# A hybrid encoder layer: near scores multiplied in pairs, a shorter second norm, three subtractions queued later

## The chip, the cores and the metric

The kernel runs on one core of one Trainium2 chip. The core has five engines with a queue each, worked off in order: TensorE (PE; its weight loads are shown apart as PEld), VectorE (DVE), ScalarE (ACT), GpSimd (POOL) and SyncE (SP), which here only issues transfers. TensorE writes into PSUM, a small memory of eight banks of 2 KB per partition; the other data lie in SBUF, and large ones in device memory. The metric is the device time of one launch in microseconds (us), lower is better.

## The reference

The input x has 1024 positions of 1024 features. One layer is computed, in float32:

```
u = RMSNorm(x);  p = u @ W_in               split into attention and delta-rule parts
A: 8 heads of 64, chunks of 64 positions; each chunk attends to itself and the 8 chunks before it
   scores = q k^T / 8 + bias[clipped distance];  softmax;  o_att = RMSNorm(P v)
B: 4 heads of 128: causal convolution, SiLU, gated delta-rule recurrence over chunks, gated RMSNorm
h = x + concat[o_att, B] @ W_out
h = h + relu(RMSNorm(h) @ W1)^2 @ W2        W1 is 1024 x 4096, W2 is 4096 x 1024
```

The second RMSNorm divides each position by sqrt(mean(h^2) + EPS). Because the activation is relu squared, the kernel can multiply its result by 1 / (mean(h^2) + EPS) after the activation instead: a plain reciprocal, no root.

## The kernel before, in words

The positions are columns and the features are rows of 128. Each float32 operand of the large products is split into a high part (a cast on ScalarE, L149) and a low part (a subtraction on VectorE or GpSimd, L150), and each product is three matmuls: high by high, high by low, low by high.

The work goes through these stages. The projections by W_in come first (to about 363 us). Then attention and the delta rule run side by side (to about 575 us): two Python generators hand out pieces in turn, and each piece's instructions enter the program in that order. Then comes the product with W_out (to 661 us), the first feed-forward product (to 974 us) and the second (to the end). The order of each engine's queue is not the program's order alone: a planner at compile time works through the program with a model of durations, gives each engine the ready instruction that stands first in the program, and adds the semaphore waits. The kernel bends that order with two means. `tc.issue_after(ins)` queues what is traced inside it behind `ins` on the same engine, with no wait added; `tc.high_priority()` lets it go before other ready work.

**Attention.** A unit is one group of four heads (g), one block of 128 positions (t) and one pair of heads (pp). `score` (from L795) first handles the near keys, that is the own block of 128 and the one before it. For each of the two heads, `product` writes two matmuls per block of keys into one half of one PSUM bank (t_sb), and VectorE adds the bias, writes the result to SBUF and takes the negated minimum of the negated scores in the same instruction (L810, t_nm). Then come the far keys, one bank per head (t_sa, L819), with the near minimum as start value, and ScalarE's exponentials (L825, L828). `value` transposes them on TensorE (t_tpb, t_tpa), copies them out (t_tb, t_ta) and multiplies by the values (t_o).

**The second norm.** `norm_col` (from L1036) loads the sums of squares, already added up over the rows of features except for the last 128, and sums these by matmuls with a column of ones, one column of result per block of 128 positions (hcol). VectorE turns that into mean plus EPS (L1045) and takes the reciprocal (L1047) into r_col, behind an addition of the second column block (held). `norm_row` (L1049) spreads r_col along rows by matmuls with an identity (hrow), and ScalarE copies them out as r2 (L1055), with which every result of the first feed-forward product is multiplied (emit, L1097).

**The second feed-forward product.** `ff2` computes seven products instead of eight per round (Strassen's scheme in Winograd's form), in four rounds over the rows of W2 (kb from 0 to 3), in the order p1, p5, p2, p3, p6, p7, p4. Each product takes sums or differences of quarters of the operands as input, made on VectorE:

```
prep5: s1 = a21 + a22;    b11 = b12 - b11        (L1263, L1264)
prep3: s1 = s1 - a11;     a12 = a12 - s1         (L1268, L1269)
prep6: b11 = b22 - b11                           (L1273)
prep7: a21 = a11 - a21;   b12 = b22 - b12        (L1277, L1278)
prep4: b21 = b11 - b21                           (L1282)
```

Each runs twice per product, on pieces of 128 x 1024 (i is 0 or 1). Then the operands are split, and 48 matmuls follow (L1185). Names such as p50b_l say: product 5, round 0, operand b, low part. The results are added to y on VectorE (L1253) or copied on ScalarE (L1251).

Of the kernel before, what the change touches and what calls it, by code (L numbers as in the profile page):

```python
# [8 lines left out]
F32 = mybir.dt.float32  # L9
F32R = mybir.dt.float32r  # L10
AF = mybir.ActivationFunctionType
ALU = mybir.AluOpType
AX = mybir.AxisListType

P = 128
SEQ = 1024
DM = 1024
NKT = DM // P
NT = SEQ // P
# [9 lines left out]
EPS = 1e-6  # L29
# [17 lines left out]
def hymba_kernel(  # L47
# [20 lines left out]
    nc = tc.nc  # L68
    PS = bass.MemoryType.PSUM

    cpool = ctx.enter_context(tc.tile_pool(name="cpool", bufs=1))
# [29 lines left out]
    def bank(pool, name):  # L101
        return pool.tile([P, 512], F32, tag="bk", name=name)
# [4 lines left out]
    ones = cpool.tile([P, P], F32, name="ones")  # L107
# [3 lines left out]
    warm = bank(ps_o, "warm")  # L111
    for i in range(WARM):
        nc.tensor.matmul(warm[:, 0:P], ones, ones, start=True, stop=True)
    ident = cpool.tile([P, P], F32, name="ident")
    make_identity(nc, ident)
    tri_u = mpool.tile([P, P], F32, name="tri_u")
# [31 lines left out]
    def split(src, hi, lo, hi_eng, lo_eng):  # L148
        a = nc.scalar.copy(hi, src) if hi_eng is nc.scalar else hi_eng.tensor_copy(hi, src)  # L149
        return a.ins, lo_eng.tensor_tensor(lo, src, hi.bitcast(F32), ALU.subtract).ins  # L150
# [21 lines left out]
    r_col = cpool.tile([P, NT], F32, name="r_col")  # L172
# [535 lines left out]
    def attention(after):  # L708
# [74 lines left out]
        def product(g, T, i, bk, off, ka, kb):  # L783

            q = T["q"]
            cost = 0
            for hf in range(2):
                a, b = max(ka, 4 * hf), min(kb, 4 * hf + 4)
                if a >= b:
                    continue  # L790
                k = keys[g][hf][i]
                o = bk[:, off + (a - ka) * P:off + (b - ka) * P]
                c = slice((a - 4 * hf) * P, (b - 4 * hf) * P)
                for m in range(2):
                    nc.tensor.matmul(o, q[m][:, i * P:(i + 1) * P], k[:, c], start=(m == 0), stop=(m == 1))  # L795
                cost += max(214, (b - a) * 107)
            return cost

        def score(g, t, pp):
            T = tiles[g, t]  # L800
            n, k0, kb, nm = (T[k] for k in ("n", "k0", "kb", "nm"))
            wa, wb = (kb - k0) * P, (t + 1 - kb) * P
            cost = 0
            bk = bank(ps_a, f"{n}_sb{pp}")
            sb = page("u" if g or t > 1 else "wr", f"{n}_pb{pp}")
            for e in range(2):
                i = 2 * pp + e
                c = slice(e * 256 + 256 - wb, e * 256 + 256)
                cost += product(g, T, i, bk, c.start, kb, t + 1)
                nc.vector.tensor_tensor_reduce(sb[:, c], bk[:, c], new[g][pp][:, c], -1.0, 3.0e38,  # L810
                                               ALU.add, ALU.min, nm[:, 4 + i:5 + i])
            sa = [None, None]
            if wa:
                for e in range(2):
                    i = 2 * pp + e
                    bk = bank(ps_a, f"{n}_sa{i}")
                    cost += product(g, T, i, bk, 0, k0, kb)
                    sa[e] = page("u", f"{n}_pa{i}")
                    nc.vector.tensor_tensor_reduce(sa[e][:, 0:wa], bk[:, 0:wa], old[g][i][:, 384 - wa:384], -1.0,  # L819
                                                   nm[:, 4 + i:5 + i], ALU.add, ALU.min, nm[:, i:i + 1])  # L820
            for e in range(2):
                i = 2 * pp + e
                c = slice(e * 256 + 256 - wb, e * 256 + 256)
                m = nm[:, i:i + 1] if wa else nm[:, 4 + i:5 + i]
                nc.scalar.activation(sb[:, c], sb[:, c], AF.Exp, bias=m, scale=-1.0,  # L825
                                     accum_out=T["sums"][:, 4 + i:5 + i])
                if wa:
                    nc.scalar.activation(sa[e][:, 0:wa], sa[e][:, 0:wa], AF.Exp, bias=m, scale=-1.0,  # L828
                                         accum_out=T["sums"][:, i:i + 1])
            T["s"][pp] = sa, sb  # L830
            return cost
# [80 lines left out]
        for i in range(len(units) + lag + late):  # L912
            if i < len(units):
                g, t, pp = units[i]
# [8 lines left out]
            if lag <= i < len(units) + lag:  # L923
                g, t, pp = units[i - lag]
# [3 lines left out]
            if i >= lag + late:  # L928
                g, t, pp = units[i - lag - late]
# [69 lines left out]
    def ff1(R, started, psw, pools):  # L999
# [4 lines left out]
        r2 = pools["r2"][0].tile([P, 2, TH], F32, tag="r2", name="r2", bufs=1)  # L1004
        begun, held = {}, []
# [31 lines left out]
        def norm_col():  # L1037

            acc = page2("ut4", "acc")
            nc.sync.dma_start(out=acc, in_=sq_dr)  # L1040
            ps = psw.tile([P, 1024], F32, tag="bk", name="hcol")
            for q in range(NT):
                nc.tensor.matmul(ps[:, q:q + 1], acc[:, q * P:(q + 1) * P], ones[:, 0:1], start=True, stop=True)
            with tc.issue_after(held[-1][2]):
                m = nc.vector.tensor_scalar(r_col, ps[:, 0:NT], 1.0 / DM, EPS, ALU.mult, ALU.add)  # L1045
                with tc.issue_after(m.ins), tc.high_priority():
                    nc.vector.reciprocal(r_col, r_col)  # L1047

        def norm_row():  # L1049

            ps = psw.tile([P, 1024], F32, tag="bk", name="hrow")
            for q in range(NT):
                nc.tensor.matmul(ps[:, q * P:(q + 1) * P], r_col[:, q:q + 1].broadcast_to([P, P]), ident,
                                 start=True, stop=True)
            nc.scalar.copy(r2.rearrange("p a t -> p (a t)"), ps)  # L1055

        def block(sb):
            def lw(tag, name, kh, c):
# [102 lines left out]
    def ff2(psw, pools):  # L1161
# [7 lines left out]

        y = {i: [wide(t, 0), wide(t, 1)] for i, t in y.items()}  # L1170
        y[7] = [page2("y7", f"y7_{i}") for i in range(2)]
        side = [0]

        def load_h(t, j, hf, m):
            nc.sync.dma_start(out=two(t), in_=h_dr[j, hf, :, 2 * m:2 * m + 2, :])
# [1 line left out]
        def product(name, prep, by_rows=False):  # L1177
            t = "AB"[side[0]]
            side[0] ^= 1
            ps = [psw.tile([P, 1024], F32, tag="bk", name=f"{name}{m}") for m in range(4 if by_rows else 2)]  # L1180
            def step(i, k, q):
                (ah, al), (bh, bl) = ops[i]
                s = slice(k * 512 + q * P, k * 512 + (q + 1) * P)
                for m, (l, r) in enumerate(((ah, bh), (ah, bl), (al, bh))):
                    nc.tensor.matmul(part(ps[q], 0) if by_rows else part(ps[q // 2], q % 2), l[:, s], part(r, k),  # L1185
                                     start=(i + k + m == 0), stop=(i + k + m == 4))

            ops = []
            for i in range(2):
                ab = []  # L1190
                for o, src in zip("ab", prep(i)):
                    hi = page2("h" + t, f"{name}{o}{i}_h", F32R)
                    lo = page2("l" + t, f"{name}{o}{i}_l", F32R)
                    split(src, hi, lo, nc.scalar, nc.vector)
                    ab.append((hi, lo))
                ops.append(ab)
                if not by_rows:
                    for k in range(2):
                        for q in range(4):
                            step(i, k, q)  # L1200
            if by_rows:
                for q in range(4):
                    for i in range(2):
                        for k in range(2):
                            step(i, k, q)
            return ps
# [7 lines left out]
        for kb in range(nb):  # L1214
# [18 lines left out]
            a11, b11 = wq("r", "a11", k1, 0), fq("r", "b11", k1, 0)  # L1233
            a21, a22, b12 = wq("rc", "a21", k1, 1), wq("rc", "a22", k2, 1), fq("rc", "b12", k1, 1)
# [11 lines left out]
            s1 = []  # L1246

            def accumulate(i, ps, op=ALU.add):
                for m in range(2):
                    if kb == 0 and i in (1, 5, 6, 7):  # L1250
                        nc.scalar.copy(y[i][m], ps[m])  # L1251
                    else:
                        nc.vector.tensor_tensor(y[i][m], y[i][m], ps[m], op)  # L1253
# [5 lines left out]
            tt = nc.vector.tensor_tensor  # L1259
# [5 lines left out]
                return s1[i], b11[i]  # L1265

            def prep3(i):
                tt(s1[i], s1[i], a11[i], ALU.subtract)  # L1268
                tt(a12[i], a12[i], s1[i], ALU.subtract)  # L1269
                return a12[i], b22[i]  # L1270

# [2 lines left out]
                return s1[i], b11[i]  # L1274

            def prep7(i):
                tt(a21[i], a11[i], a21[i], ALU.subtract)  # L1277
                tt(b12[i], b22[i], b12[i], ALU.subtract)  # L1278
                return a21[i], b12[i]

# [3 lines left out]

            accumulate(1, product(f"p1{kb}", lambda i: (a11[i], b11[i])))
            accumulate(5, product(f"p5{kb}", prep5))
            accumulate(2, product(f"p2{kb}", lambda i: (a12[i], b21[i])))
            if last:
                merge(nc.gpsimd, 2, 1)
# [16 lines left out]
            ps = product(f"p4{kb}", prep4, last)  # L1306
# [3 lines left out]
            for q in range(4):  # L1310
                t = part(y[4][q // 2], q % 2)
# [98 lines left out]
```

## Time and profile before

| | us |
|---|---|
| median of 3 runs | 1286.36 (1286.24 to 1288.97) |
| the profiled execution's own time | 1286.66 |
| its span in the profile | 1284.9 |
| TensorE busy | 1259.1 |
| VectorE busy | 935.3 |
| ScalarE busy | 554.4 |
| GpSimd busy | 292.8 |

The span runs from the first to the last instruction of the profiled execution; its own time also holds the start and end of the launch. Busy time of TensorE counts from a matmul's start to its modelled end, so neighbouring matmuls overlap in it. In rows of the profile in order of time stand start, duration, engine, line, operation, output and inputs by name, shape and count; in brackets the engine's idle time before it and what ended it. Several like instructions in a row are merged into one row with a count.

### The profile page before, as it was taken

What the parts mean: (1) busy time and instruction counts of PE and PEld (TensorE: products, weight loads), DVE (VectorE), ACT (ScalarE), POOL (GpSimd) and SP (SyncE); (2) the same over time, 40 slices, a digit from 0 to 9 for tenths busy, and PEclk for the clock granted to TensorE, in tenths of its full rate; (3) what the DMA queues carried; (4) which work ended last, traced back from release to release, by engine and by line L of the source; (5) the groups of instructions that cost most, each with busy time, mean ns of one, the idle gap of its engine ahead of it and who ended that gap; (6) DMA issues with size and microseconds to landing.
All of it is one profiled execution on the core that took longest, in us unless ns stands there. A gap on an engine that the chain in (4) does not pass through costs nothing.

```text
span 1284.9 us, 18056 instructions
## 1 busy us (share of the span) xinstructions
PE 1259.1 (98%) x6708; PEld 1039.7 (81%) x6708; DVE 935.3 (73%) x1401; ACT 554.4 (43%) x920; POOL 292.8 (23%) x499
## 2 busy tenths in 40 slices
PE   9999999999999999989999999999999999999998
PEld 7778878788888877868877788888887888888886
DVE  7899987655046666863539876776668997897988
ACT  7323132133166654665335455444455443333331
POOL 4425451454024355523310000000000000000034
PEclk9999999999999999999999999999999999999999
DMA  6214354656482642124341433232258633322002
GB/s 223 65 43 142 98 160 118 139 147 164 144 267 81 216 108 75 42 67 163 127 160 37 144 121 125 99 113 99 99 196 323 233 97 101 131 87 95 15 33 98
DMA packets 129288, 160.65 MB, mean 125 GB/s; under 512 B 22832, under 2 KB 71984, under 8 KB 128688
## 3 DMA queue, kind: packets, MB, share of 16 engines
q1 hardware_dynamic: 111104, 137.20, 34.6%
q10 hardware_dynamic: 18096, 22.29, 5.0%
q8 instruction: 53, 0.87, 0.3%
q14 instruction: 35, 0.29, 0.1%
HBM read 111.75 MB, written 47.71 MB: 124 GB/s over the span
## 4 chain that ended last, share of the span: by engine, by line
PE 72%; DVE 9%; DMA 2%; issue 2%; ACT 1%; POOL 1%; POOLq 1%; SPq 0%; DVEq 0%; ACTq 0%
PE q L1089 22%; PE p L1185 20%; PE op L168 5%; PE av_ps L168 3%; PE aq_ps L168 3%; PE g_ps L168 3%; PE t_o L867 2%; PE ak_ps L168 2%; PE t_sb L795 1%; PE t_sa L795 1%; PE t_tpb L846 1%; PE t_tpa L857 1%; PE c_mt L463 1%; PE c_pS L463 1%; DVE ml L150 1%
## 5 line engine op out<-in xcount | busy, mean ns | idle before, releaser
L1257 POOL TENSOR_TENSOR y<-y,y 128x1024 f32<-128x1024 f32 x6 | 19.3, 3242 | 591.7 <-DVE y L1253 572.9
L1253 DVE TENSOR_TENSOR y<-y,p 128x1024 f32<-128x1024 f32 x46 | 55.0, 1214 | 5.4 <-PE p L1185 4.5
L810 DVE CUSTOM_DVE_ANT_0 t_pb<-t_sb,biasn 128x256 f32<-128x256 f32 (+1 forms) x64 | 25.3, 401 | 42.9 <-POOL biasn L722 25.5
L168 PE MATMUL op<-mh,wo_h 128*128 128x512 f32 x128 | 50.3, 393 | 1.0 <-ACT wo_h L149 0.5
L168 PE MATMUL op<-ml,wo_h 128*128 128x512 f32 x128 | 50.1, 391 | 0.0
L168 PE MATMUL op<-mh,wo_l 128*128 128x512 f32 x128 | 48.3, 392 | 0.0
L825 ACT ACTIVATE t_pb<-t_pb,t_nm 128x256 f32<-128x256 f32 (+1 forms) x64 | 31.5, 493 | 22.2 <-DVE t_nm L819 12.1
L968 DVE TENSOR_TENSOR h<-op,op_x 128x512 f32<-128x512 f32 x16 | 10.8, 687 | 29.5 <-PE op L168 29.5
L795 PE MATMUL t_sb<-ks,t_q 128*128 128x256 f32 (+1 forms) x144 | 30.4, 308 | 1.3 <-DMA t_q<-q_dr 1.1
L975 POOL TENSOR_TENSOR op_q<-op_q 128x512 f32<-128x512 f32 x14 | 20.1, 1438 | 47.0 <-ACT op_q L974 46.8
L168 PEld LDWEIGHTS op<-mh,wo_h 128*128 128x128 f32 x128 | 24.1, 188 | 7.6 <-issue 1.0
L819 DVE CUSTOM_DVE_ANT_0 t_pa<-t_sa,biaso,t_nm 128x384 f32<-128x384 f32 (+2 forms) x48 | 26.3, 547 | 4.4 <-PE t_sa L795 2.9
L168 PEld LDWEIGHTS op<-mh,wo_l 128*128 128x128 f32 x128 | 24.0, 188 | 5.2 <-issue 0.2
L168 PEld LDWEIGHTS op<-ml,wo_h 128*128 128x128 f32 x128 | 24.0, 188 | 4.9
L867 PE MATMUL t_o<-t_ta,vt 128*64 128x128 f32 x240 | 26.5, 286 | 1.4 <-DVE t_ta L860 1.1
L828 ACT ACTIVATE t_pa<-t_pa,t_nm 128x384 f32<-128x384 f32 (+2 forms) x48 | 26.4, 550 | 0.1
L168 PE MATMUL g_ps<-uh,wg_h 128*128 128x512 f32 x64 | 25.2, 394 | 1.1 <-ACT wg_h L149 1.1
L795 PE MATMUL t_sa<-ks,t_q 128*128 128x256 f32 (+2 forms) x128 | 25.5, 311 | 0.3 <-DVE t_nm L810 0.3
L168 PE MATMUL g_ps<-uh,wg_l 128*128 128x512 f32 x64 | 25.2, 394 | 0.4 <-POOL wg_l L150 0.4
L168 PE MATMUL dq_ps<-uh,wdq_h 128*128 128x512 f32 x64 | 25.5, 398 | 0.0
L168 PE MATMUL dv_ps<-uh,wdv_l 128*128 128x512 f32 x64 | 25.4, 398 | 0.0
L168 PE MATMUL aq_ps<-waq_h,uh 128*128 128x512 f32 x64 | 25.4, 401 | 0.0
(1103 smaller groups left out, 4351.2 us busy)
## 6 DMA issues: line engine op xcount, KB each, us to landing
wa<-in_w_ff_dram SPq DMA_DIRECT2D x32, 512.0 KB
a<-in_w_ff_dram SPq DMA_DIRECT2D x32, 512.0 KB
b<-f_dr SPq DMA_DIRECT2D x32, 512.0 KB
f_dr<-yy ACTq DMA_DIRECT2D x16, 512.0 KB
t_q<-q_dr SPq DMA_DIRECT2D x30, 256.0 KB
f_dr<-zz ACTq DMA_DIRECT2D x13, 512.0 KB
ks<-k_dr SPq DMA_DIRECT2D x16, 256.0 KB
wo_r<-in_w_out_dram SPq DMA_DIRECT2D x16, 256.0 KB
```

The costliest lines, as they stand in the source:

```text
L168: nc.tensor.matmul(ps, a, b, start=(i == 0), stop=(i == n - 1))
L463: nc.tensor.matmul(ps[:, hs], lhs(h, hs), rhs(h, hs), start=True, stop=True)
L795: nc.tensor.matmul(o, q[m][:, i * P:(i + 1) * P], k[:, c], start=(m == 0), stop=(m == 1))
L810: nc.vector.tensor_tensor_reduce(sb[:, c], bk[:, c], new[g][pp][:, c], -1.0, 3.0e38, ALU.add, ALU.min, nm[:, 4 + i:5 + i])
L819: nc.vector.tensor_tensor_reduce(sa[e][:, 0:wa], bk[:, 0:wa], old[g][i][:, 384 - wa:384], -1.0, nm[:, 4 + i:5 + i], ALU.add, ALU.min, nm[: ...
L825: nc.scalar.activation(sb[:, c], sb[:, c], AF.Exp, bias=m, scale=-1.0, accum_out=T["sums"][:, 4 + i:5 + i])
L828: nc.scalar.activation(sa[e][:, 0:wa], sa[e][:, 0:wa], AF.Exp, bias=m, scale=-1.0, accum_out=T["sums"][:, i:i + 1])
L867: nc.tensor.matmul(po[64 * e:64 * e + 64, pp * P:(pp + 1) * P], vt[k0 + j][:, 64 * h:64 * h + 64], (ta[e] if j < na else tb)[:, c:c + P], ...
L975: nc.gpsimd.tensor_tensor(acc, acc, sq, ALU.add)
L1089: nc.tensor.matmul(part(ps, q), l[:, s], r, start=(k + m == 0), stop=(k == 3 and m == 2))
L1185: nc.tensor.matmul(part(ps[q], 0) if by_rows else part(ps[q // 2], q % 2), l[:, s], part(r, k), start=(i + k + m == 0), stop=(i + k + m == 4))
L1253: nc.vector.tensor_tensor(y[i][m], y[i][m], ps[m], op)
```

## The change

Four edits are made together.

In `score`, the loop over the two heads is cut into two: first both near products are issued, then both minima are taken.

In `norm_col`, a tile epsc filled with EPS * 1024 / 128 (one memset on GpSimd at the start) is multiplied by a matrix of ones, which adds EPS * 1024 to each column of the sum; the nine products become one accumulation. The reciprocal is then taken straight from PSUM, in one VectorE instruction with high priority, and the factor 1024 that the mean lacks is put into ScalarE's copy of the rows.

In `ff2`, each low-part subtraction is remembered, and `early` is the last one of product 5. The subtractions s1 - a11 of product 3 and a11 - a21 of product 7 are queued behind it.

```
+    epsc = cpool.tile([P, NT], F32, name="epsc")
+    nc.gpsimd.memset(epsc, EPS * DM / P)
...
                 cost += product(g, T, i, bk, c.start, kb, t + 1)
+            for e in range(2):
+                i = 2 * pp + e
+                c = slice(e * 256 + 256 - wb, e * 256 + 256)
                 nc.vector.tensor_tensor_reduce(sb[:, c], bk[:, c], new[g][pp][:, c], -1.0, 3.0e38,
                                                ALU.add, ALU.min, nm[:, 4 + i:5 + i])
...
+            nc.tensor.matmul(ps[:, 0:NT], ones, epsc, start=True, stop=False)
             for q in range(NT):
-                nc.tensor.matmul(ps[:, q:q + 1], acc[:, q * P:(q + 1) * P], ones[:, 0:1], start=True, stop=True)
-            with tc.issue_after(held[-1][2]):
-                m = nc.vector.tensor_scalar(r_col, ps[:, 0:NT], 1.0 / DM, EPS, ALU.mult, ALU.add)
-                with tc.issue_after(m.ins), tc.high_priority():
-                    nc.vector.reciprocal(r_col, r_col)
+                nc.tensor.matmul(ps[:, q:q + 1], acc[:, q * P:(q + 1) * P], ones[:, 0:1], start=False, stop=q == NT - 1)
+            with tc.issue_after(held[-1][2]), tc.high_priority():
+                nc.vector.reciprocal(r_col, ps[:, 0:NT])
...
-            nc.scalar.copy(r2.rearrange("p a t -> p (a t)"), ps)
+            nc.scalar.mul(r2.rearrange("p a t -> p (a t)"), ps, float(DM))
...
-                    split(src, hi, lo, nc.scalar, nc.vector)
+                    splits.append(split(src, hi, lo, nc.scalar, nc.vector)[1])
...
             def prep3(i):
-                tt(s1[i], s1[i], a11[i], ALU.subtract)
+                with tc.issue_after(early):
+                    tt(s1[i], s1[i], a11[i], ALU.subtract)
...
             def prep7(i):
-                tt(a21[i], a11[i], a21[i], ALU.subtract)
+                with tc.issue_after(early):
+                    tt(a21[i], a11[i], a21[i], ALU.subtract)
...
             accumulate(5, product(f"p5{kb}", prep5))
+            early = splits[-1]
```

More of the change, by code (lines that the diff above doesn't have):

```diff
@@ L1171, in ff2 @@
         y[7] = [page2("y7", f"y7_{i}") for i in range(2)]
-        side = [0]
+        side, splits = [0], []
         def load_h(t, j, hf, m):
```

## The prediction

> **What bounds the kernel now.** I read the page first, then the busy time by stretch, then TensorE's waits, and last the instructions in order of time around the three places that the change touches. The page:
>
> ```profile
> span 1284.9 us, 18056 instructions
> PE 1259.1 (98%) x6708; PEld 1039.7 (81%) x6708; DVE 935.3 (73%) x1401; ACT 554.4 (43%) x920; POOL 292.8 (23%) x499
> PE 72%; DVE 9%; DMA 2%; issue 2%; ACT 1%; POOL 1%; POOLq 1%; SPq 0%; DVEq 0%; ACTq 0%
> ```
>
> TensorE is busy for 98% of the span and holds 72% of the chain of waits; VectorE holds 9% of it. So an edit can only win where TensorE stands still (1284.9 - 1259.1 = 25.8 us in all), or where it shortens TensorE's own work. Busy time by stretch (columns: length, then TensorE, its weight loads, VectorE, ScalarE, GpSimd with instruction counts):
>
> ```profile
> 480.00:520.00 40.00, 37.30 (x359) 31.73 (x358) 27.25 (x78) 20.61 (x61) 21.59 (x55) 1.00 0.21 61
> 520.00:560.00 40.00, 37.98 (x342) 32.93 (x340) 33.94 (x95) 28.82 (x80) 17.89 (x53) 1.00 0.13 34
> 560.00:580.00 20.00, 17.05 (x112) 12.91 (x111) 10.40 (x19) 9.74 (x25) 6.04 (x10) 1.00 0.43 132
> 990.00:1245.00 255.00, 255.00 (x1127) 211.22 (x1126) 226.24 (x194) 102.68 (x103) 5.75 (x2) 1.00 0.33 109
> ```
>
> The end of the attention part (480 to 580 us) holds 2.70 + 2.02 + 2.95 = 7.7 us of standstill, and the second product of the feed-forward part, from 990 us on, holds none. TensorE's waits, with total, times and longest:
>
> ```profile
> PE p L1185 <- DVE p50b_l L150: 1.8, 1, 1.8
> PE hrow L1053 <- DVE r_col L1047: 1.6, 1, 1.6
> PE t_sa L795 <- DVE t_nm L810: 0.3, 1, 0.3
> PE t_sb L795 <- DVE t_nm L810: 0.2, 1, 0.2
> ```
>
> The two longest waits of the kernel are at the places that the second norm and the differences touch. The waits of the score products on the minima (t_nm) are 0.5 us together.
>
> **Three differences (L1268, L1277).** They lie at the start of the second feed-forward product. VectorE there, in order of time (start, duration):
>
> ```profile
> 976.88 1.22 DVE L1277 TENSOR_TENSOR a<-a,a 128x1024 f32<-128x1024 f32 x1
> 979.16 1.22 DVE L1264 TENSOR_TENSOR b<-b,b 128x1024 f32<-128x1024 f32 x1
> 980.29 1.22 DVE L1277 TENSOR_TENSOR a<-a,a 128x1024 f32<-128x1024 f32 x1
> 983.70 1.22 DVE L1268 TENSOR_TENSOR s<-s,a 128x1024 f32<-128x1024 f32 x1
> 984.83 1.22 DVE L150 TENSOR_TENSOR p50b_l<-b,p50b_h 128x1024 fp32r<-128x1024 f32 x1
> 988.24 1.22 DVE L150 TENSOR_TENSOR p50b_l<-b,p50b_h 128x1024 fp32r<-128x1024 f32 x1
> 990.95 1.23 DVE L150 TENSOR_TENSOR p20b_l<-b,p20b_h 128x1024 fp32r<-128x1024 f32 x1 [1.50 <-ACT p20b_h L149]
> ```
>
> ScalarE and TensorE beside it:
>
> ```profile
> 980.47 1.05 ACT L149 CAST p50b_h<-b 128x1024 fp32r<-128x1024 f32 x1 [2.44 <-DVE b L1264]
> 983.71 0.61 PE L1185 MATMUL p<-p50b_h,p50a_h 128*128 128x512 f32 x2
> 986.11 0.50 PE L1185 MATMUL p<-p50b_l,p50a_h 128*128 128x512 f32 x1 [1.79 <-DVE p50b_l L150]
> ```
>
> TensorE begins p5 at 983.71, does two matmuls at 0.23 each, would go on at 984.17, and goes on at 986.11, when VectorE has ended p50b_l (984.83 + 1.22 = 986.05). That is 1.94 us lost. Before p50b_l stand two subtractions of L1277 and one of L1268, which products 7 and 3 need, not p5. The change queues them behind the last low part of p5 (988.24). From 979.16 to 980.29 VectorE spends 1.13 per instruction, so three fewer put p50b_l at 984.83 - 3.4 = 981.43. Its other input allows that: the cast p50b_h on ScalarE (980.47) follows L1264 of 979.16, which moves up 1.13 with the first L1277, so the cast ends near 980.4. p50b_l would end at 982.65, 1.5 us before TensorE asks for it. I take the whole 1.9 us. The trace shows only that the data of L1264 had landed by 979.16, not when; were it only just there, L1264 keeps its place and p50b_l runs from 982.6 to 983.8, still in time. The lower end is 0: the order is written at compile time, and other ready VectorE work can fill the three freed places; two (such as the low parts of p20a and of the second p50a) would leave p50b_l at 983.7, TensorE at 985.0 and a gain of 1.1.
>
> Where the moved work goes: behind 988.24, which itself moves to 984.8. VectorE then has a gap until 990.95, where p20b_l waits 1.50 us for ScalarE; the gap grows to 990.95 - 986.1 = 4.9 us and takes the three (3.4 us). Cost nothing; without that gap it is up to 3.4 us on VectorE. What is late next is the low part of p3:
>
> ```profile
> 1010.26 1.21 DVE L150 TENSOR_TENSOR p30b_l<-b,p30b_h 128x1024 fp32r<-128x1024 f32 x1
> 1013.44 0.39 PE L1185 MATMUL p<-p30b_l,p30a_h 128*128 128x512 f32 x1
> ```
>
> It ends at 1011.47 and is used at 1013.44, or 1011.5 when TensorE is 1.9 us earlier: just in time even if VectorE gains nothing. In the later three rounds the same constraint moves three subtractions of 1.2 us behind p5's low parts; there VectorE runs far ahead:
>
> ```profile
> 1075.30 1.22 DVE L150 TENSOR_TENSOR p31b_l<-b,p31b_h 128x1024 fp32r<-128x1024 f32 x1
> 1089.37 0.39 PE L1185 MATMUL p<-p31b_l,p31a_h 128*128 128x512 f32 x1
> ```
>
> The low part ends at 1076.5, 12.9 us before its use; 3.4 us more do not reach TensorE.
>
> **The second norm (L1043 to L1055).** VectorE and TensorE:
>
> ```profile
> 692.75 0.15 DVE L1045 TENSOR_SCALAR r_col<-hcol 128x8 f32<-128x8 f32 x1
> 692.82 1.21 DVE L150 TENSOR_TENSOR q_0a_l<-wa,q_0a_h 128x1024 fp32r<-128x1024 f32 x1
> 697.36 0.18 DVE L1047 RECIPROCAL r_col<-r_col 128x8 f32<-128x8 f32 x1
> 683.16 1.84 PE L1043 MATMUL hcol<-ones,acc 128*128 128x1 f32 x16
> 695.66 0.39 PE L1089 MATMUL q<-t2h,q_0a_l 128*128 128x512 f32 x1
> 697.70 2.02 PE L1053 MATMUL hrow<-ident,r_col 128*128 128x128 f32 x16 [1.65 <-DVE r_col L1047]
> 708.78 1.21 DVE L150 TENSOR_TENSOR q_1a_l<-ws,q_1a_h 128x1024 fp32r<-128x1024 f32 x1
> 711.17 0.39 PE L1089 MATMUL q<-t1h,q_1a_l 128*128 128x512 f32 x1
> 724.51 1.22 DVE L1125 TENSOR_TENSOR yy<-yy,q 128x1024 f32<-128x1024 f32 x1 [3.18 <-PE q L1089]
> ```
>
> The multiply-add at 692.75 goes: 0.07 of VectorE's time (692.82 follows). Its constants move into an extra product of ones with epsc (L1043's group: 16 records from 683.16 to about 684.86, 0.106 each, two per product, so 0.21 us more on TensorE) and into ScalarE's scaled copy, where it costs nothing because TensorE doesn't wait for r2. epsc's memset is one more of GpSimd's first instructions; the nearest row, a memset of 16 columns, takes 0.11:
>
> ```profile
> 1.07 0.11 POOL L128 MEMSET mhalf<- 128x16 f32 x1
> 5.41 1.27 POOL L150 TENSOR_TENSOR wdk_l<-wdk_r,wdk_h 128x512 fp32r<-128x512 f32 x1 [2.86 <-ACT wdk_h L149]
> ```
>
> GpSimd then idles 2.86 us, which hides it. The reciprocal is the real edit: it stands at 697.36, five places behind the multiply-add, and the row product hrow starts at 697.70 after 1.65 us of standstill. With one instruction instead of two, the reciprocal can take the place at 692.75, since what it needs (hcol) is what the multiply-add needed. TensorE would go from 695.66 to hrow at 695.89 instead of 697.70: 1.81 won, less 0.21 gives 1.60. But not all of it lasts. VectorE has no idle time until 724.51, and its low part q_1a_l ends at 708.78 + 1.21 = 709.99; the matmul that reads it starts at 711.17. That is 1.18 us of room, plus 0.07 that VectorE gains. I take 1.2 us. Bounds: 1.6 if the order of VectorE's work improves too, -0.2 if the reciprocal stays where it is.
>
> **The near scores (L805 to L813).** Two matmuls per head (L795), then the minimum (L810):
>
> ```profile
> 407.47 0.51 PE L795 MATMUL t_sb<-ks,t_q 128*128 128x256 f32 x2
> 408.01 0.42 DVE L810 CUSTOM_DVE_ANT_0 t_pb<-t_sb,biasn 128x256 f32<-128x256 f32 x1 [0.48 <-PE t_sb L795]
> 410.69 0.51 PE L795 MATMUL t_sb<-ks,t_q 128*128 128x256 f32 x2
> 544.67 1.33 PE L795 MATMUL t_sa<-ks,t_q 128*128 128x256 f32 x8 [0.29 <-DVE t_nm L810]
> ```
>
> Nothing is added or removed: 64 products and 64 minima stay. Before, both heads' columns lie in one bank, and the second head's product stands in the queue behind the first head's minimum; here they are at 407.47 and 410.69, with other TensorE work between them. After, the products are neighbours, and one exchange between TensorE and VectorE per pair falls away, 32 in all. The direct price is what TensorE waits for these minima now, 0.5 us; I take half, 0.3 rounded. Against it, the first minimum starts one product later: two matmuls take 0.51 and eight of the same width 1.33, so (1.33 - 0.51) / 6 = 0.14 for each further one and 0.28 for a product. Since the whole order of this part is made anew, the bounds are wide: 7.7 us of standstill from 480 to 580 us could shrink by some 3, an estimate from the stretch that ends the part (2.95), or grow by as much as 32 x 0.28 = 9.0.
>
> By the Trainium skill, page "PSUM — Partial Sum Buffer", section "PSUM bank collisions raise a hardware error", two engines must be kept apart by bank, not by address. It speaks against this edit: the first minimum can't run beside the second product although it reads other columns. The sum by it is the slower rival below; the trace so far agrees in that 0.2 us of wait by the second product on the minimum is listed.
>
> **Sum.** 1.9 + 1.2 + 0.3 = 3.4 us. The profiled execution took 1286.66 us (span 1284.9 and 1.76 around it), 0.3 above the median of 1286.36 shown. 1286.66 - 3.4 = 1283.3, and against the median 1283.0; I forecast 1283.0.
>
> **Rivals.**
> - Only one of the two joins pays: other VectorE work fills the freed places, or the reciprocal stays behind low parts. For it: before, the reciprocal stood five places late for no reason that the profile shows. Against: three instructions are bound to come later. 1.9 or 1.2 remains, less 0.2: about 1285.0.
> - The new order of the attention part also wins some of the 7.7 us, say 3: 1280.0. For it: waits at the end (560 to 580 us) are chains from scores to exponentials, each shortened by an exchange. Against: the direct waits are 0.5 us.
> - Slower: the first minimum waits for the second product and TensorE has nothing in between. Price 0.28 per pair; with 20 of 32 it is 5.6, less the joins' 3.1: 2.5 more than 1286.5, so 1289.0. It decides once more than 11 pairs (3.1 / 0.28) stand on TensorE's path. For it: VectorE is at 33.94 of 40 us from 520 to 560. Against: TensorE had other work between the products.
> - The change doesn't do what it says: the compile-time order hides all of it, 1286.5.
>
> **How the numbers follow.** Forecast 0.44 (own range 1281.5 to 1284.5), one join 0.20, attention wins 0.15, slower 0.10, nothing 0.11. About 0.2% (2.6 us) is what a measurement of this kernel can tell from no change; so faster means under 1283.8. Of the forecast's 0.44 some 0.36 lies below that, with 0.15 from the attention case: faster 0.51. Slower, over 1288.9, gets 0.11 (its case, spread up to all 32 pairs, and a little of the others), the rest is 0.38. The range 1279.5 to 1287.3 leaves out most of the slower case and the tail of the attention case.
>
> **What would show it.** Right: no wait of p (L1185) on p50b_l, L1268 and L1277 behind p5's low parts, one reciprocal near 692 us and no wait of hrow, near-score matmuls in groups of four, and the stretch 990 to the end as long as before. Wrong: p50b_l still after 984, hrow waiting for r_col, a new wait at q_1a_l longer than 0.5 us, or more standstill from 480 to 580 us than 7.7.

## The result, and the profile after

The changed kernel takes 1292.40 us (median of 8 runs, 1289.04 to 1298.35), the kernel before 1287.44 us beside it (8 runs, 1286.24 to 1290.56). The ratio is 1.0042, its 95% interval 1.0024 to 1.0060: slower by 0.4%, where the prediction had 1283.0 and 0.51 for faster. The profiled execution of the changed kernel took 1295.24 us, with a span of 1293.4; before it was 1284.9.

The page of the changed kernel, the rows that answer to those of before (lines of the code stand 2 to 6 higher, so L1185 is now L1189, L795 is L797, L1053 is L1057, L150 is L152):

```profile
span 1293.4 us, 18062 instructions
PE 1266.3 (98%) x6710; PEld 1044.7 (81%) x6710; DVE 931.9 (72%) x1400; ACT 553.5 (43%) x920; POOL 292.7 (23%) x500
PE 70%; DVE 7%; DMA 6%; issue 2%; ACT 2%; POOL 1%; POOLq 1%; SPq 0%; ACTq 0%; DVEq 0%
```

TensorE is busy 7.2 us longer (1266.3 against 1259.1), although it has only two matmuls more; DMA now has 6% of the chain instead of 2%. The two waits that were the longest are gone, and two others stand in their place:

```profile
PE p L1189 <- DVE p30b_l L152: 4.7, 1, 4.7
PE t_sb L797 <- DMA t_q<-q_dr: 3.1, 1, 3.1
```

By stretch (length, then busy time of TensorE, its weight loads, VectorE, ScalarE, GpSimd, with counts; then the granted clock, DMA share, GB/s), first of the changed kernel, then the one row of before that was not shown yet:

```profile
363.00:400.00 37.00, 33.90 (x289) 28.30 (x288) 17.06 (x69) 19.37 (x63) 9.23 (x18) 0.86 0.57 168
480.00:580.00 100.00, 94.39 (x838) 79.76 (x837) 73.11 (x206) 62.76 (x180) 47.46 (x126) 1.00 0.23 65
990.00:1245.00 255.00, 249.40 (x1092) 205.41 (x1091) 220.32 (x192) 101.83 (x103) 0.28 (x1) 0.99 0.32 109
```

```profile
363.00:400.00 37.00, 37.00 (x364) 31.24 (x363) 20.71 (x81) 23.70 (x76) 11.47 (x24) 1.00 0.63 193
```

The late part of the attention has less standstill than before (100.00 - 94.39 = 5.6 us from 480 to 580, before 7.7, although the work has moved by 2 to 3 us in this stretch). The loss is at two other places: 363 to 400 us, where TensorE was never idle before and now is for 3.1 us with a granted clock of 0.86, and behind 990 us, where the prediction said "as long as before".

**The first place, 373 us.** TensorE and SyncE in order of time (start, duration; in brackets the idle time before and what ended it):

```profile
362.98 2.27 SPq L739 DMA_DIRECT2D ks<-k_dr  x4
365.61 1.17 SPq L778 DMA_DIRECT2D t_q<-q_dr  x2
376.01 0.91 PE L797 MATMUL t_sb<-ks,t_q 128*128 128x256 f32 x4 [3.10 <-DMA t_q<-q_dr]
372.93:376.35 3.42, 0.34 (x3) 0.37 (x4) 0.36 (x2) 1.19 (x5) 0.00 (x0) 1.00 1.00 321
376.35:386.59 10.24, 10.24 (x52) 8.42 (x51) 2.84 (x12) 2.54 (x6) 0.53 (x1) 0.50 0.33 81
```

The group of four near-score matmuls of unit (0, 3) stands in TensorE's queue ahead of the landing of its query load (t_q), which SyncE issues at 365.61 behind four key loads that nothing needs yet. TensorE stands for 3.10 us from 372.91 on, and then works for 10.24 us at half clock. Before, counted back from the first group of 128 x 128, the unit's first product stood at 376.20, 3.3 us later, and waited for nothing.

**The second place, the norm.** The wait of hrow on r_col is gone, as forecast. But hcol's sixteen matmuls moved, and behind them the clock is at half for 3.41 us:

```profile
691.08 1.84 PE L1049 MATMUL hcol<-ones,acc 128*128 128x1 f32 x16
700.46 1.72 PE L1057 MATMUL hrow<-ident,r_col 128*128 128x128 f32 x14
695.88 0.20 DVE L1051 RECIPROCAL r_col<-hcol 128x8 f32<-128x8 f32 x1
693.79:697.20 3.41, 3.41 (x8) 2.73 (x9) 3.41 (x5) 3.25 (x4) 0.00 (x0) 0.50 0.54 154
```

The row product hrow starts 2.76 us later than before (697.70), of which some 2.3 come from the attention part (the first product of this part starts at 663.6, before at 661.32): the norm has won nothing here and lost 0.5.

**The third place, p2 and p3 of the second feed-forward product.** ScalarE, VectorE and TensorE:

```profile
993.42 0.37 ACTq L1102 DMA_DIRECT2D f_dr<-yy  x1
993.89 1.01 ACT L1255 COPY y<-p 128x1024 f32<-128x1024 f32 x1 [8.95 <-DMA y<-h_dr]
994.80 1.05 ACT L151 CAST p20a_h<-a 128x1024 fp32r<-128x1024 f32 x1
```

```profile
995.88 1.23 DVE L152 TENSOR_TENSOR p20a_l<-a,p20a_h 128x1024 fp32r<-128x1024 f32 x1 [3.77 <-ACT p20a_h L151]
1007.96 2.35 DVE L1288 TENSOR_TENSOR b<-b,b 128x1024 f32<-128x1024 f32 x2
1010.23 1.22 DVE L152 TENSOR_TENSOR p60a_l<-s,p60a_h 128x1024 fp32r<-128x1024 f32 x1
1013.64 1.22 DVE L152 TENSOR_TENSOR p30b_l<-b,p30b_h 128x1024 fp32r<-128x1024 f32 x1
```

```profile
986.36 0.61 PE L1189 MATMUL p<-p50b_h,p50a_h 128*128 128x512 f32 x2
1014.91 0.79 PE L1189 MATMUL p<-p30b_l,p30a_h 128*128 128x512 f32 x1 [4.72 <-DVE p30b_l L152]
1014.64:1018.05 3.41, 3.14 (x7) 2.48 (x8) 3.41 (x4) 0.00 (x0) 0.00 (x0) 0.50 0.92 292
```

p5 runs from 986.36 without a wait. But ScalarE does nothing for 8.95 us, to 993.89: it stands before the issue of a write (f_dr<-yy, L1102), which waits until a load with which it shares no data, y<-h_dr, has landed. The cast p20a_h stands behind it, VectorE idles 3.77 us for that, and then makes b21 for p4 (L1288, two instructions) and the low parts of p6 before those of p3. Of p3's low parts p30b_l is made twice, once for each half of the operand, and the first one is late. Before, it stood ahead of the second of b21's two instructions and of p6's low parts, and ended at 1005.79, 2.2 us before its use (1008.00):

```profile
1004.58 1.21 DVE L150 TENSOR_TENSOR p30b_l<-b,p30b_h 128x1024 fp32r<-128x1024 f32 x1
```

Now it ends at 1014.86; TensorE has waited 4.72 us for it, and half clock follows for 3.41 us. From p5's start (2.65 us late) to the end (8.5 us late) 5.85 us are lost.

**Why TensorE's busy time grew.** The half clock stretches of this execution sum to 10.24 + 3.41 + 3.41 = 17.06 us, so the work done in them took some 8.5 us more than at full clock; the kernel before has no such stretch until its last microseconds. How many there are seems to differ from run to run: the eight runs go from 1289.04 us at a mean granted clock of 0.998 to 1298.35 at 0.991.

### The profile page after: what moved, and what is told of

Read it like the earlier page. It is cut to its first block, busy times and chain, and to the rows that moved or that the text cites. A ratio compares the mean times of both kernels' runs of the same rounds, so it can differ in the third digit from the quotient of the medians.

```text
span 1293.4 us, 18062 instructions
## 1 busy us (share of the span) xinstructions
PE 1266.3 (98%) x6710; PEld 1044.7 (81%) x6710; DVE 931.9 (72%) x1400; ACT 553.5 (43%) x920; POOL 292.7 (23%) x500
## 4 chain that ended last, share of the span: by engine, by line
PE 70%; DVE 7%; DMA 6%; issue 2%; ACT 2%; POOL 1%; POOLq 1%; SPq 0%; ACTq 0%; DVEq 0%
PE q L1093 21%; PE p L1189 19%; PE op L170 4%; PE aq_ps L170 3%; PE av_ps L170 3%; PE g_ps L170 3%; PE t_o L872 2%; PE ak_ps L170 2%; PE t_sa L797 1%; PE t_sb L797 1%; PE t_tpb L851 1%; PE t_tpa L862 1%; DMA wo_r<-in_w_out_dram 1%; DMA y<-h_dr 1%; DMA t_q<-q_dr 1%
## 5 line engine op out<-in xcount | busy, mean ns | idle before, releaser
L854 ACT COPY t_tb<-t_tpb 128x512 f32<-128x512 f32 (+1 forms) x32 | 17.8, 557 | 26.1 <-PE t_tpb L851 26.0
L797 PE MATMUL t_sb<-ks,t_q 128*128 128x256 f32 (+1 forms) x144 | 24.0, 294 | 3.1 <-DMA t_q<-q_dr 3.1
L797 PE MATMUL t_sa<-ks,t_q 128*128 128x256 f32 (+2 forms) x128 | 26.0, 312 | 0.0
```

## The experiments

My theory after this comparison: the three edits lose or win at their own places, and two queue orders (a load on SyncE, a write on ScalarE) with VectorE's new order make the waits. Rival 1: one edit causes all, by shifting the rest; rival 2: the slow clock is chance, and the edits do nothing. By the order of instructions on each engine, the near-score edit changes the attention part alone, while the norm's edit also moves a few instructions in the second product, so that the edits aren't quite independent.

**Each edit alone, and two of them.**

Only the near scores (the second hunk of the change):

> Only the near-score edit; the second norm and the differences as before. Theory (each edit costs at its own place): 2 us slower than before, about 1288.5 to 1290; TensorE waits about 3 us for the query load of a unit near 373 us, the granted clock is 0.5 for some 10 us after it, and hcol, hrow and the wait on p50b_l (about 1.8 us) are as before. Rival 1 (the near scores alone cause all of it, by shifting what follows): 5 us slower, about 1292, with the new wait on p30b_l too. Rival 2 (the slow clock is chance and the edits do nothing): 1286.5 to 1287.5.

Measured 1288.36 us, ratio 1.0002 (0.9989 to 1.0016).

```profile
375.44 0.71 PE L795 MATMUL t_sb<-ks,t_q 128*128 128x256 f32 x4 [2.30 <-DMA t_q<-q_dr]
373.51:376.93 3.42, 1.49 (x13) 1.29 (x14) 0.07 (x3) 0.98 (x4) 0.00 (x0) 1.00 1.05 318
376.93:387.17 10.24, 10.24 (x54) 8.22 (x52) 4.06 (x15) 3.97 (x10) 2.01 (x3) 0.50 0.30 73
```

The wait and the 10.24 us at half clock are there; the wait on p50b_l is 1.8 us as before, and none on p30b_l is listed: rival 1 falls. On average nothing is won or lost, where the theory had a loss of 2 us. But two of the eleven runs had a mean clock of 1.000 and took 1283.35 and 1283.54 us; the other nine, at 0.994 to 0.998, took 1285.84 to 1290.81. The nine runs of before at a clock of 0.999 have a median of 1286.39. So the edit seems to have a gain of some 3 us, and the stall with its half clock takes it away.

Only the norm (epsc, the accumulation, the reciprocal, the scaled copy):

> Only the second norm's edit. Theory: hrow's wait of 1.6 us goes, but what is won is lost again at the next low parts or in a stretch at half clock near 693 us: 1286.5 to 1287.5, no difference that can be told. Rival 1 (the near scores alone cause the loss): the 1.2 us of the prediction, 1285 to 1286. Rival 3 (the norm's half clock decides and recurs): 1288 to 1289, the clock 0.5 for 3.4 us behind hcol's products.

Measured 1285.85 us, ratio 0.9990 (0.9982 to 0.9999).

```profile
660.48 0.47 PE L1090 MATMUL q<-b11h,q_0a_h 128*128 128x512 f32 x1 [0.88 <-DVE h L970]
695.30 1.95 PE L1054 MATMUL hrow<-ident,r_col 128*128 128x128 f32 x16
981.60 0.61 PE L1186 MATMUL p<-p50b_h,p50a_h 128*128 128x512 f32 x2
```

At the first product this execution is 0.84 us ahead of the one before (660.48 against 661.32), at hrow 2.40 (697.70), at p5 2.11 (983.71). So the norm wins 1.56 us at hrow, of which 1.27 are left at p5: the prediction's 1.6 and 1.2. Then p2 waits 0.4 us for p20b_h, and 0.6 reach the end of this execution (a span of 1283.5 against 1284.9, less the 0.84 from before the norm). My theory of no gain falls; rival 1's number was right, for another reason.

Only the three differences:

> Only the three differences are queued behind the last low part of p5. Theory: the wait on p50b_l (1.8 us) goes, a wait of 4 to 5 us on p30b_l near 1010 us takes its place, some with a stretch at half clock behind it: 1289 to 1292. Rival 1 (the near scores alone, whose later arrival makes the stall): no wait on p30b_l over 0.5 us, 1284 to 1285. Rival 2 (nothing): 1286.5 to 1287.5.

Measured 1293.70 us, ratio 1.0054 (1.0042 to 1.0066), above the theory's 1289 to 1292.

```profile
984.50 0.61 PE L1185 MATMUL p<-p50b_h,p50a_h 128*128 128x512 f32 x2
1007.65 0.61 PE L1185 MATMUL p<-p30b_h,p30a_h 128*128 128x512 f32 x2
993.96 1.23 DVE L150 TENSOR_TENSOR p20a_l<-a,p20a_h 128x1024 fp32r<-128x1024 f32 x1 [3.70 <-ACT p20a_h L149]
PE p L1185 <- DVE p30b_l L150: 4.7, 1, 4.7
```

```profile
1007.54 0.62 PE L1185 MATMUL p<-p30b_h,p30a_h 128*128 128x512 f32 x2
```

This execution starts p5 0.79 us later than the one before, and p3 0.11 later: of the 1.94 us that p5's wait held, 0.7 is left at p3's start. Then p3 loses, and the span ends 6.7 us later (1291.6). The edit alone costs about as much as the whole change (1.0042, 1.0024 to 1.0060); the near scores have no part in it.

The norm and the differences:

> The norm and the differences, without the near scores. Theory: the sum of the two single ones, 1289 to 1292, with the wait on p30b_l and without one on a query load near 373 us. Rival 1: 1283.5 to 1285, faster than before by the prediction's 3.1 us or a part of it. Rival 2: 1286.5 to 1287.5.

Measured 1292.62 us, ratio 1.0043 (1.0030 to 1.0056). The single ratios give 0.9990 + 0.0054 = 1.0044. With the near scores' 0.0002 this is 1.0046, beside the whole change's 1.0042: within the noise the edits add up.

**What makes the stall at p3.** All three kernels contain the differences alone. In the first, VectorE's differences for p6, p7 and p4 and the low parts of p6 are queued behind p3's last low part:

```
             def prep7(i):
...
-                tt(b12[i], b22[i], b12[i], ALU.subtract)
...
+                with tc.issue_after(third):
+                    tt(b12[i], b22[i], b12[i], ALU.subtract)
...
             def prep4(i):
-                tt(b21[i], b11[i], b21[i], ALU.subtract)
+                with tc.issue_after(third):
+                    tt(b21[i], b11[i], b21[i], ALU.subtract)
...
             accumulate(3, product(f"p3{kb}", prep3))
-            accumulate(6, product(f"p6{kb}", prep6))
+            third = splits[-1]
+            with tc.issue_after(third):
+                accumulate(6, product(f"p6{kb}", prep6))
```

> The three differences as in the run with them alone, and what p6, p7 and p4 need on VectorE (two differences each, and p6's low parts) queued behind the last low part of p3. ScalarE's order is not touched. Theory (VectorE's new order makes the stall at p3): eight instructions of 1.13 us that stood ahead of p30b_l come later, so that it ends near 1004 instead of 1012.9 and TensorE, which asks for it at about 1008, does not wait: no wait on p30b_l, no half clock near 1013, and the 6.5 us lost between the end of p2 and the end of p3 come back; the short waits on p20's parts stay. About 1287. Rival (the transfer that blocks ScalarE's queue is the whole cause): p3 still waits 3 us or more, 1291 to 1293.

Measured 1288.37 us, ratio 1.0006 (0.9997 to 1.0015), where the theory had about 1287. p3 waits no more, and the profile has no half clock before its last microseconds. TensorE's times are 0.68 us ahead of before from p2's end on, yet the span is 1.8 us longer. The lost part is at the end, where VectorE's last merges of products start 1.73 us later, because the new order holds in the last round too (the last experiment, with the first round alone, doesn't lose this), and GpSimd's sum for the output follows them. First this kernel, then the one before:

```profile
1273.62 4.62 DVE L1257 TENSOR_TENSOR y<-y,y 128x1024 f32<-128x1024 f32 x4
```

```profile
1271.89 4.61 DVE L1257 TENSOR_TENSOR y<-y,y 128x1024 f32<-128x1024 f32 x4
```

In the second, the write that blocks ScalarE is issued by GpSimd:

```
-                nc.scalar.dma_start(out=f_dr[sb * 4 + fh * 2:...
+                q = nc.gpsimd if (sb, fh, th) == (DFF // FB - 1, 1, 0) else nc.scalar
+                q.dma_start(out=f_dr[sb * 4 + fh * 2:...
```

> The three differences, and the last write of the first product's result is issued by GpSimd instead of ScalarE, so that nothing on ScalarE stands behind its wait. VectorE's order stays but for one place. Theory (both causes add up): the waits on p20's parts (0.4 and 0.5 us by the waits, 1.85 us by TensorE's times) go, VectorE idles 2.8 us less ahead of p20a_l, and p30b_l comes 2.8 us earlier; TensorE still waits 3 to 4 us for it: 1289 to 1291. Rival (the blocked queue is the whole cause): no wait on p30b_l over 0.5 us, 1285 to 1286. Rival (VectorE's order alone): no gain, 1293.

Measured 1285.98 us, ratio 0.9991 (0.9983 to 1.0000).

```profile
981.13 0.97 POOL L1099 DMA_DIRECT2D f_dr<-yy  x1 [318.50 <-DVE yy L1097]
983.01 0.62 PE L1186 MATMUL p<-p50b_h,p50a_h 128*128 128x512 f32 x2
1004.77 0.39 PE L1186 MATMUL p<-p30b_h,p30a_h 128*128 128x512 f32 x1
1005.71 1.23 DVE L150 TENSOR_TENSOR p30b_l<-b,p30b_h 128x1024 fp32r<-128x1024 f32 x1
PE p L1186 <- DVE p30b_l L150: 1.6, 1, 1.6
```

This one line takes away 7.7 us by the medians (1293.70 to 1285.98) and 8.1 by the ratios, more than the theory's 1289 to 1291 allows. All of VectorE's 4.3 us of idle time before p2's low parts (3.70 before p20a_l, 0.63 before p20b_l) is gone, where I had counted 2.8, the part beyond before's 1.50; and no half clock follows the wait of 1.6 us that is left. GpSimd issues the write 0.3 us after its data (980.82), and ScalarE's two copies run at 982.44 without waiting for y<-h_dr, so it was the write's issue on ScalarE that had waited for that load. The rival's time was right, but its reason only in part: the wait on p30b_l is still there. Either mend by itself takes most of the stall away: p3 waits for nothing with VectorE's order mended and the queue still blocked, and 1.6 us with the queue free. The 4.7 us needed both causes, and these runs don't say which of them is the larger.

Both together:

> Both of these with the three differences. Theory: the 2.5 us that p5 wins against before (984.50 to 995.55 without a wait) reach the end: 1285 to 1285.5, no wait at p5, p2 or p3 over 0.5 us. Rival (something else of VectorE's or the transfers' is late next): 1287 or more.

Measured 1286.38 us, ratio 0.9994 (0.9986 to 1.0003). No wait stands in the second product, and TensorE reaches p3 at 1004.93, 2.61 us ahead of before, but the late merges at the end give 2.3 of that back, as in the first of the three. The time lies between the theory's 1285 to 1285.5 and the rival's 1287 or more; what the rival says holds, with the merges as what is late next.

**What the near scores win.** The query load of unit (0, 3) goes ahead of the value and key loads that stood before it on SyncE:

```
                     if (g, t) == (0, 2):
                         load_rest()
+                        start(0, 3)
+                        with tc.issue_after(qld[0, 3]):
+                            load_late()
```

where `load_late` is the part of `load_rest` that loads values 4 to 7 and the second group's keys, and `qld` keeps the load's instruction.

> The near-score edit alone, with the query load of unit (0, 3) issued on SyncE's queue ahead of three value loads and of the four key loads of the second group of heads, which follow it. Theory: the wait of 2.3 to 3.1 us for that load near 373 us goes, the 10 us at half clock behind it go too (5 us of work), and most of that reaches the end of the attention part: 1282 to 1286. Rival (the late part of the attention, 440 to 580 us, decides whatever happens here): 1287.5 to 1289, though the wait is gone. Rival (another load becomes the late one, since the transfers are busy all the time here): a wait of 2 us or more at another tile, with the half clock again, 1288 to 1290.

Measured 1282.80 us, ratio 0.9964 (0.9949 to 0.9978): 4.6 us faster than before by the ratio, and 5.6 faster than the near scores with the late load by the medians (4.9 by the ratios).

```profile
363.00:400.00 37.00, 36.86 (x360) 31.02 (x358) 21.52 (x82) 23.24 (x76) 10.70 (x23) 1.00 0.64 191
440.00:480.00 40.00, 39.88 (x398) 34.42 (x396) 22.54 (x80) 25.16 (x80) 17.90 (x49) 1.00 0.46 120
480.00:520.00 40.00, 38.31 (x357) 33.07 (x356) 28.18 (x81) 21.76 (x65) 19.32 (x52) 1.00 0.28 74
```

There is no wait for a load, and the clock is 1.00. TensorE begins the first feed-forward product at 656.13 instead of 661.32. From 440 to 520 us TensorE stands 1.8 us (0.12 + 1.69) instead of 4.2 (1.51 and 2.70, from 38.49 and 37.30 busy of 40). Is it the load's place that wins? The same in the kernel before:

> The kernel before, with nothing of the change, and the query load of unit (0, 3) issued ahead of the value and key loads as in the run with the near scores and this load. It tells whether the 4.6 us won there come from the load's place or from the near scores behind it. Theory (the pairs win, once their load is early): 1286 to 1287.5, no difference to before. Rival (the load's place alone wins): 1282 to 1284.

Measured 1285.26 us, ratio 0.9985 (0.9975 to 0.9995): 1.7 us, between my two cases. This is not a clean control, since the planner made a new order of the attention part for it, and of a piece of the first feed-forward product. There is a wait of 2.2 us on another query load, with 3.41 us at half clock behind it (456.13):

```profile
PE t_sb L797 <- DMA t_q<-q_dr: 2.2, 1, 2.2
```

By TensorE's times the attention part ends 0.6 us later than before in this execution, so what it gains isn't from there: it goes from 0.5 us behind at hrow (698.24) to 0.7 ahead at p5 (983.04), in the first feed-forward product. But the wait and its half clock cost 2.2 + 1.7 = 3.9 us, and without them, by this sum, the attention part would have ended some 3 us earlier than before. The load's place alone, as measured, does not explain the 4.6 us; how much of it the paired products win by themselves stays open.

**The whole change with its causes mended, one after the other.** The load ahead:

> The whole change, and this load ahead. Theory (the losses of the places add up): the 5.6 us between the two runs with the near scores alone come off: 1286 to 1288, with no wait for a query load near 373 us, no half clock there, and the wait of 4.7 us on p30b_l still there. Rival (the wait on p30b_l hangs on when the part starts, as the loads of the second product are busy then): another size of that wait, 3 us or 6 us and more.

Measured 1287.66 us, ratio 1.0003 (0.9993 to 1.0013). The wait on p30b_l is 4.7 us as before the mend, so it doesn't hang on when the part starts.

The load ahead and the write issued by GpSimd:

> The whole change, this load ahead, and the last write of the first product's result issued by GpSimd. Theory: 7 us less than without the write's move, 1279 to 1281.5; a wait of about 1.6 us on p30b_l stays. Rival (a stretch at half clock behind hcol's products near 690 us belongs to the norm's edit and comes back): the clock 0.5 for 3.4 us there, 1281 to 1283.

Measured 1281.11 us, ratio 0.9952 (0.9939 to 0.9964), with a wait of 1.6 us on p30b_l, and at full clock until its last microseconds: no half clock behind hcol.

And p6, p7 and p4 behind p3 in the first round only (the contexts of the first experiment on p3, empty unless kb is 0):

> As the one before, and in the first of the four rounds of the second product what p6, p7 and p4 need on VectorE queued behind p3's last low part. Theory: the wait of 1.6 us on p30b_l goes too, and the end of the kernel stays as long as before, since the last round isn't touched: 1277.5 to 1280. Rival (another low part is late next): the same time as without it, with a wait elsewhere in the second product.

Measured 1278.85 us (1277.83 to 1280.55), ratio 0.9933 (0.9920 to 0.9946): by the ratio 8.6 us faster than before, and by the medians 13.6 faster than the change as it was. No wait in the second product is left, and the end is as long as before; one stretch of 3.41 us at half clock stands behind hcol (686.12). The longest wait of the kernel is now far ahead of all this:

```profile
PE ak_tp L434 <- DVE ak_n L429: 1.2, 1, 1.2
```

## Why the prediction was wrong, point by point

**The differences.** Right: p50b_l came in time, and the 1.9 us of p5 were there to be won. With the write on GpSimd TensorE is 0.70 us ahead of before at p5's start (983.01) and 2.77 at p3's (1004.77), so 2.07 were won by then. But in the sum the term of 1.9 us came out as a loss of 7 (1.0054). The step that failed is "the gap grows to 990.95 - 986.1 = 4.9 us and takes the three (3.4 us). Cost nothing", together with "just in time even if VectorE gains nothing". The moved instructions did run in the gap (from 987.49 on in the changed kernel), but VectorE stood still for longer behind them than before. The gap before p20b_l ended with a cast on ScalarE, and I asked neither what held that cast nor whether ScalarE's order would stay. The trace of before had the answer:

```profile
982.37 1.05 ACT L149 CAST p20a_h<-a 128x1024 fp32r<-128x1024 f32 x1
989.46 0.37 ACTq L1098 DMA_DIRECT2D f_dr<-yy  x1
989.87 1.05 ACT L149 CAST p20b_h<-b 128x1024 fp32r<-128x1024 f32 x1 [3.69 <-DVE p50b_l L150]
```

The same write stands before p20b_h there (the second row), ScalarE idle, but p20a_h and two copies had gone ahead of it. In the new order these stand behind it, and VectorE, which needs p20a_h, stands with them. The price was 3.77 + 0.63 us of VectorE's idle time instead of 1.50, and 3.4 us for three instructions (the second of b21's and p6's two low parts) that the planner now puts ahead of the first p30b_l: 6.3 us together. Against that stood 2.2 us of room, less the 0.6 us that TensorE had won by then (2.65 us late at p5's start, 2.03 at p3's): 4.7 us of wait, as measured. The low part of p3 was named as the next late one, with zero slack, and zero slack was priced at zero; the prediction looked at the second p30b_l (1010.26), while the first, which became late, had 0.3 us by the same reckoning (1008.00 - 1.9 - 1005.79). Beside the wait, the half clock behind it cost 1.6 us in the change (half of 3.14 us of work) and 2.6 in the run with the load ahead (half of 5.19).

**The norm.** Right in mechanism, and in size at its place: 1.56 us at hrow and 1.27 left at p5, forecast 1.6 and 1.2; 0.9990 as a time. That p2 waits longer afterwards wasn't foreseen, nor the new place of hcol's products, behind which the half clock took the gain away in the change.

**The near scores.** The forecast of 0.3 us stands beside 0.2 us slower (1.0002, no difference that can be told), but it hides two things that were missed: a gain (some 3 us in the two runs at full clock, 4.6 with the load ahead, of which the load's place may have a part), and a stall of 2.3 to 3.1 us with 10.24 us at half clock that takes it away. The step "The direct price is what TensorE waits for these minima now" put a price on the exchange alone, and not on what the products' new place in the queue asks of the loads. The rival "the new order of the attention part also wins" was right that there is a gain. The slower rival (the first minimum waits for the second product) does not show: the waits of t_sa and t_sb on the minima (0.3 and 0.2 us before) are no longer listed in the changed kernel. The Trainium skill's rule behind that rival (page "PSUM — Partial Sum Buffer", section "PSUM bank collisions raise a hardware error") cost nothing that these runs show.

**The rivals and the range.** 1292.4 lies above the range (1287.3). The one slower case had the wrong mechanism; a wait that takes the place of the one removed stood in my text as a check ("what is late next") and not as a rival with a price.

## What to carry to other kernels

Taking work out from before a wait can change the order of engines that the edit doesn't name (here ScalarE's and TensorE's beside VectorE's), so ask of each gap you mean to use what ends it, and what would stand behind that if it came one place earlier; a transfer's issue on a computing engine holds all that is queued behind it. An input with no slack is a rival and needs a price. A stall of TensorE costs its length and, in the profiles here from 2.2 us on, a stretch at half clock behind it.

## What was not expected of the hardware

Between the first moment at full clock and the last microseconds of the kernel, every stretch at half clock in these fourteen profiles lasts 3.413 us or two or three times that, and starts a whole number of 3.413 us after that first moment. All seven single waits of TensorE from 2.18 to 4.72 us have one behind them, and none of the fifteen from 1.60 to 1.79 us (most of them hrow's and p5's). What TensorE did in the 3.41 us before seems to decide. Busy time in such a window, first one in the attention part of the kernel with the differences alone, at whose end the clock fell, then one at hrow in the kernel with the near scores alone, at whose end it did not:

```profile
548.68:552.09 3.41, 1.75 (x14) 1.34 (x14) 1.70 (x6) 2.51 (x8) 1.50 (x6) 1.00 0.00 0
```

```profile
697.78:701.19 3.41, 1.62 (x14) 1.35 (x13) 3.41 (x5) 1.16 (x2) 0.00 (x0) 1.00 0.02 5
```

So a window need not be empty: 1.66 us of standstill, in two waits of 0.87 and 0.80, were enough in the first. Nor is it the busy time alone that counts, since the second has less of it (1.62 against 1.75 us); where the limit lies stays open. By the times of the first full clock (3.9 to 7.2 us from the start) the windows aren't tied to the program. So a stall may fall into one window or be shared by two, and may cost half clock in one run and none in another, which fits the spread of the changed kernel from 1289 to 1298 us. The Trainium skill, page "TensorE: Matmul & The Clock Gate", section "Part 1: The HAM clock gate (the "warmup" mystery)", tells of a free-running window of this length, and of half rate after at least one idle window. The traces agree on the window and the rate, and differ on the second: standstill for half of a window can be enough.

One-column matmuls seem to count for little as work. Behind hcol's sixteen the clock fell twice, once in the changed kernel (693.79) and once in the last experiment; the windows before each, and one in which the same sixteen lie without any idle time and the clock stayed:

```profile
690.37:693.79 3.42, 3.17 (x23) 2.58 (x21) 3.42 (x4) 3.42 (x4) 0.00 (x0) 1.00 0.00 0
```

```profile
682.71:686.12 3.41, 3.30 (x23) 2.68 (x23) 3.41 (x5) 3.39 (x5) 0.00 (x0) 1.00 0.01 2
```

```profile
687.74:691.15 3.41, 3.41 (x25) 3.11 (x24) 3.41 (x4) 2.61 (x4) 0.00 (x0) 1.00 0.00 0
```

TensorE is busy for 3.17 and 3.30 of 3.4 us in the first two and for all of the last. In the run with the whole change and the load ahead a window with less, 3.07 us busy (683.14 to 686.55), kept the clock; only 1.33 us of the sixteen lie in it. That a group of 1.7 us which moves sixteen columns counts as idle, and the 0.1 to 0.25 us beside it decide, fits these four; no experiment was made on it.
